# Zero matmuls ahead of the first transposes of a hybrid attention layer, and a first phase in program order

## The chip, the cores and the metric

The kernel runs on one core of a Trainium2 chip. The metric is the device time of one launch, in microseconds. The core's engines are TensorE (PE: matmuls and transposes; its weight loads are listed apart as PEld), VectorE (DVE), ScalarE (ACT), GpSimd (POOL) and SyncE (SP, which here issues most DMAs). Each engine works through a list of its own in order; they meet through semaphores, which are counters that one raises and another waits on.

## The reference, cut to what matters

One layer over 1024 positions of width 1024. The input is normed and multiplied with a wide weight matrix, eight heads of differential attention and four heads of gated linear attention work on the parts, and an output projection, a second norm and the residual follow:

```
h = rms_norm(x, pre_g)
z = jnp.einsum('bsd,de->bse', h, w_in)          # 1024 x 1024 by 1024 x 7184
qa, ka, va, ga, qb, kb, vb, gb, gk_low = split_columns(z)
...                                             # diff. attention -> oa, gated linear attention -> ob
y = jnp.einsum('bse,ed->bsd', jnp.concatenate([oa, ob], axis=-1), w_out)
return x + rms_norm(y, post_g)
```

All is float32. Only the first line and the start of the second are touched by the change.

## The kernel before, in words

**Loads.** SP first issues four tiles of x (`load_x`, L477: 128 rows by 1024 each), the gains `pre_g`, two raw weight pieces (`load_raw`, L194), the other four x tiles (named xt), two more raw pieces and two "early" pieces (`load_early`, L236).

**Norm.** For each of the first four x tiles `norm_x` lets ScalarE square the tile and sum (L491, "junk"), ScalarE and VectorE compute the reciprocal root (`rstd`, L1480 to L1490), VectorE scales the left half of the tile (L482), and POOL later scales the right half.

**Transposes.** `first(0)` transposes the left halves of the four x tiles on TensorE (L120): each x tile gives four blocks of 128 by 128, one into each of four PSUM banks ("xT"), so that a bank is full after the fourth x tile. Then `put` makes two numbers of each bank: `h_hi` on ScalarE (L521; rounded to TensorE's fast float32 form) and `h_lo` on VectorE (L522; the rest). POOL adds both to `f1hi` (L542). `first(1)` does the same for the right halves. Weights are split in the same way: `w` by ScalarE (L315, a cast) and by VectorE (L316, the rest).

**Products.** The input projection is done as a scheme of seven products of half matrices in place of eight. `order` lists them as (pair of weight columns, number of the product); `go(n)` runs the next n through `step` and `multiply`. One product is 24 matmuls of 256 columns for the wide pairs, in three groups of eight: h_hi by w's first part, h_hi by w's second part, h_lo by w's first part, into one PSUM bank. ScalarE copies the first sum away (L427, `s`), VectorE adds pairs of sums (L403, `gv_st`). The first product is (0, 1); it needs h_hi of the first half, k = 0 to 3, one after another. After the first four products `blocks(j)` transposes the xt tiles, which POOL has scaled by then (L482 with xt), makes h_hi, h_lo (L521, L522) and their sums and differences (L565 `s`, L568, L569, L548) for the next products.

**What sets the order.** TensorE's instructions are kept in program order by `mm` and `tr` (L117 and L120 are their lines, so all matmuls carry L117 and all transposes L120). In `norm_x` for the first four tiles the other engines are kept in program order too (`pin`). Everything else on ScalarE, VectorE and POOL is ordered by a scheduler, ahead of the run. The weights of products 0 to 3 are held behind the first norm (`issue_after`, in `prepare`). PSUM banks come from the list `free`: `take_bank` takes from its front, a finished bank is appended at its end.

Of the kernel before, what the change touches and what calls it, by code (L numbers as in the profile page):

```python
# [19 lines left out]
HB = 4  # L20
# [4 lines left out]
LAM_INIT = 0.2  # L25
# [6 lines left out]
def hymba_kernel(  # L32
# [18 lines left out]


    nc = tc.nc
    act, dve, pool, pe, sp = nc.scalar, nc.vector, nc.gpsimd, nc.tensor, nc.sync

    def fp(t):
        return t.bitcast(F32)

    def cols(half):
        return slice(half * 512, half * 512 + 512)  # L60


    const = ctx.enter_context(tc.tile_pool(name="const", bufs=1))
    pre_g = const.tile([P, KT], F32, name="pre_g")
# [4 lines left out]
    ones = const.tile([P, P], F32R, name="ones")  # L69
    pool.memset(fp(ones), 1.0)  # L70

    NZ = 512
    maskt = const.tile([P, NZ + P], F32, name="maskt")
    pool.memset(maskt, 0.0)
# [6 lines left out]
    sub_g = const.tile([P, 1], F32, name="sub_g")  # L81
# [34 lines left out]
    def mm(*a, **k):  # L116
        tc.keep_in_program_order(pe.matmul(*a, **k))  # L117

    def tr(dst, src):
        tc.keep_in_program_order(pe.transpose(dst, src, ident))  # L120

    edge = ctx.enter_context(tc.tile_pool(name="edge", bufs=1, side="right"))
    pool.memset(edge.tile([P, 120], F32, name="edge"), 0.0)
    hw = ctx.enter_context(tc.tile_pool(name="hw", bufs=1, side="right", reuse_waits="tile"))
    hpool_cm = tc.tile_pool(name="hpool", bufs=1, side="right")
    hpool = hpool_cm.__enter__()

# [16 lines left out]
    def at(part, j):  # L146
        per = HB // len(part)
        return part[j // per][:, j % per]
# [32 lines left out]
    def wide(p):  # L181
        return pairs[p][0] in ("VA", "VB")
# [18 lines left out]
    n_early = len(order)  # L201
# [15 lines left out]
    i = order.index((1, 4))  # L217
# [19 lines left out]

    def prepare(i):

        if i >= len(order) or i in ws:  # L240
            return
        if i < 4:

            act_ins, dve_ins = normed[0][:2]
            with tc.issue_after(act_ins.ins), tc.issue_after(dve_ins.ins):
                make_weights(i)
        else:
            make_weights(i)
# [97 lines left out]

    decs = {}
# [132 lines left out]
    def scale_x(st, cs, engine=pool):  # L480
        x_cs = xs[st][:, cs]
        return engine.tensor_scalar(x_cs, x_cs, norms[st], 1.0, ALU.mult, ALU.mult)  # L482

    norms, normed = {}, []

    def norm_x(*sts):
        n = len(sts)
        ssq = const.tile([P, 4, n], F32, tag=f"ssq{sts[0]}", name="ssq", bufs=1)
        for i, st in enumerate(sts):
            junk = hw.tile([P, D], F32, tag=("s2_hi0", "s2_lo0")[st % 2], name="junk")  # L490
            ins = act.activation(  # L491
                junk, xs[st], AF.Square, scale=D**-0.5, accum_out=ssq[:, 0, i : i + 1]
            )
            if n == 1:
                tc.keep_in_program_order(ins)
        pin = tc.keep_in_program_order if n == 1 else None
        normed[:] = [rstd(nc, ssq[:, :, :n], ssq[:, 0, :n], eps_t, pin)]
        for i, st in enumerate(sts):
            norms[st] = ssq[:, 1, i : i + 1]
            if n == 1:  # L500
                pin(scale_x(st, cols(0), dve))
            else:
                scale_x(st, slice(0, D))

# [14 lines left out]
    def put(ps, k, dst, j):  # L519
        hi, lo = dst  # L520
        act.activation(at(hi, j), ps, AF.Copy, scale=pre_g[:, k : k + 1])  # L521
        dve.scalar_tensor_tensor(  # L522
            at(lo, j), ps, pre_g[:, k : k + 1], fp(at(hi, j)), ALU.mult, ALU.subtract
        )
# [4 lines left out]
    def first(h):  # L529

        ps = [take_bank([P, 512], "xT") for _ in range(HB)]
        for i in range(4):
            for j in range(HB):
                k = h * HB + j
                tr(ps[j][0][:, i * P : (i + 1) * P], xs[i][:, k * P : (k + 1) * P])
        hi, lo = H[("h11", "h12")[h]]
        for j in range(HB):
            put(ps[j][0], h * HB + j, (hi, lo), j)
            if h:
                act.activation(f1[h][:, j], ps[j][0], AF.Copy, scale=pre_g[:, h * HB + j : h * HB + j + 1])  # L540
            else:
                pool.tensor_tensor(f1[h][:, j], fp(at(hi, j)), fp(at(lo, j)), ALU.add)  # L542
            free.append(ps[j][1])
# [51 lines left out]
    def go(n):  # L595
        for _ in range(n):
            i = made[0]
            if i == len(order):
                return
            made[0] = i + 1  # L600
            for a in range(4):
                prepare(i + a)
            step(i)
            if order[i][0] > EARLY and not (wide(order[i][0]) and order[i][0] % 2):
                wo_step(order[i][1])
            if fill and next(fill[0], 0) == 0:
# [12 lines left out]
    for j in range(HB):  # L619
        blocks(j)  # L620
        go(1)
# [96 lines left out]


    sp.dma_start(sub_g, attn_subln_g[0].rearrange("(p o) -> p o", o=1))  # L720
    dve.tensor_scalar(sub_g, sub_g, 1.0 - LAM_INIT, None, ALU.mult)
# [255 lines left out]
    def pin(first, ins):  # L977

        if first:
            tc.keep_in_program_order(ins)  # L980
# [545 lines left out]
```

## Time and profile before

| what | us |
| --- | --- |
| median of 3 runs | 979.86 |
| lowest and highest of these | 979.69, 980.12 |
| the profiled execution, its own time | 979.08 |
| span of the profiled execution | 977.4 |
| TensorE busy, of the span | 956.7 (98%) |
| VectorE busy | 735.4 (75%) |
| ScalarE busy | 600.5 (61%) |
| POOL busy | 142.9 (15%) |

The profile is of one execution. Its views used here: the page's head (busy time of each engine); the chain that ended last, followed back from the end; the same chain in order of time (start, length, what); the timeline (start, length, engine, line, operation, out<-in, count, and in brackets the idle time before it with what ended it); the groups by form (busy time, mean ns of one, idle before); and the windows (busy time and count in stretches, the granted TensorE clock as a share of full, the DMA share, GB/s). A line such as L521 is line 521 of the kernel before; after the change the same lines stand lower.

### The profile page before, as it was taken

The page shows a single profiled execution, that of the slowest core. Times are in us where ns is not written, and L with a number is a line of the kernel's source. Part 1 is how long each engine was busy: PE and PEld are TensorE (multiplying, and loading weights), DVE is VectorE, ACT ScalarE, POOL GpSimd, SP SyncE. Part 2 cuts the span into 40 slices and gives each one's busy share as a digit, 9 for nine tenths or more (in the row PEclk, how much of TensorE's full clock was granted, in tenths as well). Part 3 has the DMA queues.
Part 4 walks back from the last instruction along what each step waited for, and adds up shares of the span by engine and source line. Part 5 has one row for each costly group of instructions (what it writes and reads, how often), then busy time and mean ns, then how long its engine had stood idle before and what let it go on. Part 6 is the DMA issues. An engine that isn't in the chain of part 4 may idle for free.

```text
span 977.4 us, 15766 instructions
## 1 busy us (share of the span) xinstructions
PE 956.7 (98%) x5338; PEld 830.4 (85%) x5338; DVE 735.4 (75%) x1452; ACT 600.5 (61%) x1164; POOL 142.9 (15%) x158
## 2 busy tenths in 40 slices
PE   5999999999999999999999999999999999999997
PEld 5998988888889998999888888878888888888785
DVE  6887597789866667686786876487888888898554
ACT  8742455487357455454665775366776687887773
POOL 4300000000000010000200002121322222443321
PEclk9999999999999999999999999999999999999999
DMA  9432446656774868897987866987656669994677
GB/s 345 151 110 91 139 135 205 231 179 225 238 247 162 264 187 286 254 294 229 293 259 243 273 202 191 407 269 272 197 186 228 240 199 344 340 294 105 151 208 147
DMA packets 152593, 220.45 MB, mean 226 GB/s; under 512 B 17104, under 2 KB 83664, under 8 KB 152416
## 3 DMA queue, kind: packets, MB, share of 16 engines
q1 hardware_dynamic: 146176, 203.71, 64.1%
q0 software_dynamic: 6336, 15.73, 7.0%
q8 instruction: 42, 0.69, 0.3%
q14 instruction: 39, 0.32, 0.1%
HBM read 133.93 MB, written 88.60 MB: 228 GB/s over the span
## 4 chain that ended last, share of the span: by engine, by line
PE 95%; DVE 2%; ACT 1%; DMA 1%; issue 1%; POOL 0%; SPq 0%; DVEq 0%; ACTq 0%; POOLq 0%
PE x L117 24%; PE y L117 15%; PE z L117 15%; PE ypart L117 13%; PE sc L117 7%; PE po L117 5%; PE yps L117 4%; PE wtr L120 3%; PE gpo L117 3%; PE kv L117 1%; PE gkl_ps L117 1%; PE pa L117 1%; DMA x<-in_x_dram 1%; PE xT L120 1%; DVE s_lo L548 0%
## 5 line engine op out<-in xcount | busy, mean ns | idle before, releaser
L315 ACT CAST w<-w_raw 128x512 fp32r<-128x512 f32 (+1 forms) x164 | 112.4, 688 | 94.7 <-PE y L117 44.1
L316 DVE TENSOR_TENSOR w<-w_raw,w 128x512 fp32r<-128x512 f32 (+1 forms) x164 | 126.7, 774 | 50.1 <-ACT w L315 43.3
L1049 ACT ACTIVATE p<-p,stt 128x896 f32<-128x896 f32 (+7 forms) x128 | 99.3, 777 | 36.7 <-DVE stt L1039 33.9
L427 ACT COPY s<-x 128x512 f32<-128x512 f32 x84 | 49.1, 585 | 84.4 <-PE x L117 84.3
L775 POOL TENSOR_SCALAR_AFFINE_SELECT gan<-gan 128x512 f32<-128x512 f32 x8 | 16.5, 2060 | 485.4 <-ACT gan L774 449.8
L296 DVE TENSOR_TENSOR w_raw<-w_raw 128x512 f32<-128x512 f32 (+1 forms) x96 | 75.9, 791 | 13.9 <-DMA w_raw<-in_w_in_dram 12.6
L1039 DVE CUSTOM_DVE_ANT_0 p<-sc,maskt 128x512 f32<-128x512 f32 (+3 forms) x128 | 74.3, 585 | 14.5 <-PE sc L117 13.3
L117 PE MATMUL ypart<-wo_hi,m_hi 128*128 128x512 f32 x192 | 79.5, 414 | 0.1
L117 PE MATMUL y<-h_hi,w 128*128 128x512 f32 x320 | 79.6, 391 | 0.0
L117 PE MATMUL z<-s_hi,w 128*128 128x512 f32 x320 | 79.6, 391 | 0.0
L117 PE MATMUL x<-s_hi,w 128*128 128x512 f32 x320 | 79.6, 391 | 0.0
L1055 POOL TENSOR_SCALAR p<-p,stt,lam 128x1024 f32<-128x1024 f32 (+3 forms) x64 | 56.2, 879 | 146.9 <-DVE stt L1054 141.9
L117 PE MATMUL ypart<-wo_hi,m_lo 128*128 128x512 f32 x192 | 75.5, 393 | 0.0
L117 PE MATMUL ypart<-wo_lo,m_hi 128*128 128x512 f32 x192 | 75.4, 393 | 0.0
L117 PE MATMUL sc<-k,q 128*128 128x512 f32 (+1 forms) x192 | 69.0, 363 | 1.3 <-DVE stt L1039 1.2
L117 PEld LDWEIGHTS x<-s_hi,w 128*128 128x128 f32 x320 | 59.7, 188 | 12.2
L117 PEld LDWEIGHTS y<-h_hi,w 128*128 128x128 f32 x320 | 59.6, 188 | 12.2
L117 PEld LDWEIGHTS z<-s_hi,w 128*128 128x128 f32 x320 | 59.5, 188 | 12.0
L117 PE MATMUL sc<-ks,q 128*128 128x512 f32 (+1 forms) x192 | 66.1, 347 | 0.0
L1097 ACT CAST wt_hi<-wtr 128x512 fp32r<-128x512 f32 (+1 forms) x80 | 42.7, 534 | 24.6 <-PE wtr L120 23.8
L1098 DVE TENSOR_TENSOR wt_lo<-wtr,wt_hi 128x512 fp32r<-128x512 f32 (+1 forms) x80 | 50.7, 633 | 8.6 <-ACT wt_hi L1097 8.0
L1058 DVE SCALAR_TENSOR_TENSOR p<-p,stt,p 128x1024 f32<-128x1024 f32 (+3 forms) x64 | 52.1, 814 | 4.1 <-POOL p L1055 3.9
(226 smaller groups left out, 2247.7 us busy)
## 6 DMA issues: line engine op xcount, KB each, us to landing
w_raw<-in_w_in_dram SPq DMA_DIRECT2D x56, 512.0 KB, 4.7
wo_raw<-in_w_out_dram SPq DMA_DIRECT2D x32, 256.0 KB, 3.0
wo_d<-wo_hi SPq DMA_DIRECT2D x32, 256.0 KB, 2.8
wo_d<-wo_raw SPq DMA_DIRECT2D x32, 256.0 KB, 3.8
q<-q_d SPq DMA_DIRECT2D x32, 256.0 KB, 4.7
k<-k_d SPq DMA_DIRECT2D x32, 256.0 KB, 5.7
ks<-k_d SPq DMA_DIRECT2D x64, 128.0 KB, 6.2
v<-v_d SPq DMA_DIRECT2D x16, 512.0 KB, 7.0
```

Of the source, the lines that this page charges most:

```text
L117: tc.keep_in_program_order(pe.matmul(*a, **k))
L120: tc.keep_in_program_order(pe.transpose(dst, src, ident))
L296: dve.tensor_tensor(dst, a, b, ALU.subtract)
L315: act.copy(w[0], src)
L316: dve.tensor_tensor(w[1], src, fp(w[0]), ALU.subtract)
L427: act.copy(b[k], ps)
L1039: ins = dve.tensor_tensor_reduce(p[:, a:e], sc[:, : e - a], maskt[:, NZ + P - (e - a) :] if last else maskt[:, : e - a], 1.0, 3e38 if i == ...
L1049: act.activation(p[:, :n], p[:, :n], AF.Exp, bias=st[:, m : m + 1], scale=-1.0, accum_out=st[:, 2 + m : 3 + m],)
L1055: pool.tensor_scalar(p1[:, :n], p1[:, :n], st[:, 5:6], lam, ALU.mult, ALU.mult)
L1058: dve.scalar_tensor_tensor(p0[:, :n], p0[:, :n], st[:, 4:5], p1[:, :n], ALU.mult, ALU.subtract)
L1097: act.copy(hi[:, :n], pt[:, :n])
L1098: dve.tensor_tensor(lo[:, :n], pt[:, :n], fp(hi[:, :n]), ALU.subtract)
```

## The change

First, TensorE gets matmuls whose result nobody reads, of a tile of ones (weights) and a tile of zeros, `idle`, 512 columns each, through a new function `spin`: ten ahead of the first transpose, then 4, 8, 4 and 5 behind the transposes of the four x tiles, and one behind every second matmul of the first eight of the first product. They go into the PSUM bank at the end of the list `free`.

Second, a wrapper (`Queue`) around ScalarE, VectorE and POOL keeps each of their instructions in program order while `pinned` is set: from the first norm to the end of `put` in `first(1)`. The norms of xt (`norm_x(4, 5)` and `norm_x(6, 7)`) and the first product move ahead of `first(1)`; the weights of products 0 to 3 are made ahead of `first(0)`; those of products 4 to 10 are held behind the last pinned instruction of ScalarE and VectorE. POOL's memsets of `ones` and `idle` become its first, and the pools `edge` and `hw` are made earlier.

In the instruction lists of the two built programs TensorE's differ by the 35 spins alone, SP's not at all, POOL's by the order of its memsets and the one for `idle`. ScalarE's and VectorE's hold the same instructions; some stand a few places from where they were, nearly all of them within the first sixty or so. Since all three engines now pass through the wrapper, their instructions carry the wrapper's line (L66) after the change, matmuls L141 and transposes L144.

```
+    pinned = [False]
+    class Queue:
...
+            def run(*a, **k):
+                ins = op(*a, **k)
+                if pinned[0]:
+                    tc.keep_in_program_order(ins)
+                    self.last = ins.ins
+                return ins
...
+    act, dve, pool = Queue(nc.scalar), Queue(nc.vector), Queue(nc.gpsimd)
...
+    ones = const.tile([P, P], F32R, name="ones")
+    pool.memset(fp(ones), 1.0)
+    idle = hw.tile([P, 512], F32R, tag="s1_hi0", name="idle")
+    pool.memset(fp(idle), 0.0)
...
-        if i < 4:
-            act_ins, dve_ins = normed[0][:2]
-            with tc.issue_after(act_ins.ins), tc.issue_after(dve_ins.ins):
+        if 4 <= i <= n_early:
+            with tc.issue_after(act.last), tc.issue_after(dve.last):
                 make_weights(i)
...
+    def spin(n):
+        for _ in range(n):
+            ps = bank(free[-1], [P, 512], "spin")
+            mm(ps, ones, idle, start=True, stop=True)
...
                         stop=(j == 2 and k == HB - 1), skip_group_check=True,
                     )
+                if i == 0 and j == 0:
+                    spin(1)
...
+    pinned[0] = True
     for st in range(4):
         norm_x(st)
...
         ps = [take_bank([P, 512], "xT") for _ in range(HB)]
+        if not h:
+            spin(10)
         for i in range(4):
             for j in range(HB):
                 k = h * HB + j
                 tr(ps[j][0][:, i * P : (i + 1) * P], xs[i][:, k * P : (k + 1) * P])
+            if not h:
+                spin((4, 8, 4, 5)[i])
         hi, lo = H[("h11", "h12")[h]]
         for j in range(HB):
             put(ps[j][0], h * HB + j, (hi, lo), j)
+        pinned[0] = not h
+        for j in range(HB):
...
-    prepare(0)
+    for i in range(4):
+        prepare(i)
     first(0)
-    for i in range(1, 4):
-        prepare(i)
-    go(1)
-    first(1)
-    go(2)
     norm_x(4, 5)
     norm_x(6, 7)
     go(1)
+    first(1)
+    go(3)
     for j in range(HB):
         blocks(j)
         go(1)
```

More of the change, by code (lines that the diff above doesn't have):

```diff
@@ L53, in hymba_kernel, with __init__, __getattr__ @@
     nc = tc.nc
-    act, dve, pool, pe, sp = nc.scalar, nc.vector, nc.gpsimd, nc.tensor, nc.sync
+    pe, sp = nc.tensor, nc.sync
+    pinned = [False]
+    class Queue:
+        def __init__(self, engine):
+            self.engine = engine
+        def __getattr__(self, name):
+            op = getattr(self.engine, name)
+            def run(*a, **k):
[4 more added lines that the diff above has]
+                return ins
+            return run
+    act, dve, pool = Queue(nc.scalar), Queue(nc.vector), Queue(nc.gpsimd)
     def fp(t):
@@ L60, in cols @@
         return slice(half * 512, half * 512 + 512)
+    edge = ctx.enter_context(tc.tile_pool(name="edge", bufs=1, side="right"))
+    hw = ctx.enter_context(tc.tile_pool(name="hw", bufs=1, side="right", reuse_waits="tile"))
     const = ctx.enter_context(tc.tile_pool(name="const", bufs=1))
+    ones = const.tile([P, P], F32R, name="ones")
+    pool.memset(fp(ones), 1.0)
+    idle = hw.tile([P, 512], F32R, tag="s1_hi0", name="idle")
+    pool.memset(fp(idle), 0.0)
+    pool.memset(edge.tile([P, 120], F32, name="edge"), 0.0)
     pre_g = const.tile([P, KT], F32, name="pre_g")
@@ L68, in hymba_kernel @@
     pool.memset(eps_t, EPS)
-    ones = const.tile([P, P], F32R, name="ones")
-    pool.memset(fp(ones), 1.0)
     NZ = 512
@@ L120, in tr @@
         tc.keep_in_program_order(pe.transpose(dst, src, ident))
-    edge = ctx.enter_context(tc.tile_pool(name="edge", bufs=1, side="right"))
-    pool.memset(edge.tile([P, 120], F32, name="edge"), 0.0)
-    hw = ctx.enter_context(tc.tile_pool(name="hw", bufs=1, side="right", reuse_waits="tile"))
     hpool_cm = tc.tile_pool(name="hpool", bufs=1, side="right")
@@ L482, in scale_x @@
         return engine.tensor_scalar(x_cs, x_cs, norms[st], 1.0, ALU.mult, ALU.mult)
-    norms, normed = {}, []
+    norms = {}
     def norm_x(*sts):
@@ L490, in norm_x @@
             junk = hw.tile([P, D], F32, tag=("s2_hi0", "s2_lo0")[st % 2], name="junk")
-            ins = act.activation(
+            act.activation(
                 junk, xs[st], AF.Square, scale=D**-0.5, accum_out=ssq[:, 0, i : i + 1]
             )
[L494 to L497, printed above, removed]
+        rstd(nc, ssq[:, :, :n], ssq[:, 0, :n], eps_t, tc.keep_in_program_order)
         for i, st in enumerate(sts):
@@ L500, in norm_x @@
             if n == 1:
-                pin(scale_x(st, cols(0), dve))
+                scale_x(st, cols(0), dve)
             else:
@@ L720, in hymba_kernel @@
     sp.dma_start(sub_g, attn_subln_g[0].rearrange("(p o) -> p o", o=1))
-    dve.tensor_scalar(sub_g, sub_g, 1.0 - LAM_INIT, None, ALU.mult)
+    tc.keep_in_program_order(dve.tensor_scalar(sub_g, sub_g, 1.0 - LAM_INIT, None, ALU.mult))
     sp.dma_start(gla_g, gla_norm_g[0].rearrange("(t p) -> p t", p=P))
```

## The prediction

> **What bounds the kernel now.** I read the page's head and its chain first, then the chain in order of time over the first 45 us, then TensorE's waits there.
>
> ```profile
> span 977.4 us, 15766 instructions
> PE 956.7 (98%) x5338; PEld 830.4 (85%) x5338; DVE 735.4 (75%) x1452; ACT 600.5 (61%) x1164; POOL 142.9 (15%) x158
> PE 95%; DVE 2%; ACT 1%; DMA 1%; issue 1%; POOL 0%; SPq 0%; DVEq 0%; ACTq 0%; POOLq 0%
> ```
>
> TensorE holds 95% of the chain that ends last. Whatever makes its first product end later or earlier moves the end of the kernel, unless a later wait of TensorE takes it up.
>
> ```profile
> 12.17 0.50 DVE x L482
> 12.67 0.04 issue
> 12.71 0.91 PE xT L120 x3
> 13.63 0.05 issue
> 13.68 0.69 ACT h_hi L521
> 14.37 0.04 issue
> 14.41 5.76 PE x L117 x24
> 20.17 1.75 PE xT L120 x16
> 21.91 2.88 PE x L117 x24
> 24.79 5.76 PE y L117 x48
> ...
> 38.91 2.89 PE y L117 x24
> 41.80 0.02 issue
> 41.83 0.69 DVE gv_st L403
> ```
>
> (Start us, length us, what.) Before 14.41 each x tile is squared, scaled and transposed; from 14.41 to 41.80 the chain is TensorE alone. The first product (24 matmuls of 256 columns) takes 5.76 us, 0.24 each; the same product in its next turn takes 2.88, 0.12 each. The 16 transposes at 20.17 take 0.11 each, the first ones about 0.22. So TensorE runs at half its rate up to about 19.8 us. The clock column doesn't show it: it says 1.00 in both of the first rows here (stretch, us, TensorE busy, clock, DMA share, GB/s), though the matmuls in 2 us (the x) go from 10 to 20.
>
> ```profile
> 16.40:18.40 2.00, 2.00 (x10) 1.00 1.06 381
> 21.80:23.80 2.00, 2.00 (x20) 1.00 1.40 455
> ...
> 975.00:976.00 1.00, 0.00 (x0) 0.00 (x0) 0.00 (x0) 0.00 (x0) 0.00 (x0) 0.77 0.60 229
> ```
>
> The column does fall at the other end, within 975 to 976, some 5 us after the last matmul. I call the two rates cold and warm. Warm came 5.4 us after the product's start at 14.41.
>
> **The change part by part: where the first product can end.** The other engines set a floor:
>
> ```profile
> 11.60 2.17 ACT L315 CAST w<-w_raw 128x1024 fp32r<-128x1024 f32 x2
> 12.66 2.77 DVE L316 TENSOR_TENSOR w<-w_raw,w 128x1024 fp32r<-128x1024 f32 x2
> 13.68 2.42 ACT L521 ACTIVATE h_hi<-xT,pre_g 128x512 fp32r<-128x512 f32 x4
> 15.35 2.71 DVE L522 SCALAR_TENSOR_TENSOR h_lo<-xT,pre_g,h_hi 128x512 fp32r<-128x512 f32 x4
> ```
>
> ScalarE's casts hold it until about 13.7, so faster transposes alone don't start h_hi earlier. VectorE is busy without a gap from 12.66 to 18.06, when the fourth h_lo is done. Both lists are in the same order in the changed program. A warm product could thus end at 18.06 plus two matmuls and a little, 18.4, against 20.17 now: 1.8 us is all that warmth can give.
>
> **The spins are not a dense stream.** In the built program each of the 31 spins before the product (10, then 4, 8, 4, 5 after the four groups of transposes) waits on TensorE's own counter for the spin before it, because all are new tiles in one bank:
>
> ```
> Matmult spin_277<-idle_66,ones_64 128x512 [waits Pool >= 2]
> Matmult spin_279<-idle_66,ones_64 128x512 [waits PE >= 1]
> Matmult spin_281<-idle_66,ones_64 128x512 [waits PE >= 2]
> ...
> Matmult x_393<-w_265,h11_hi_179 128x256
> Matmult spin_396<-idle_66,ones_64 128x512 [waits DVE >= 22]
> ```
>
> No matmul of before waits for one just ahead of it, so I bound the step of such a spin.
>
> ```profile
> 961.68 0.39 PE L117 MATMUL yps<-wo_hi,m_hi 128*128 128x512 f32 x1
> 961.91 0.39 PE L117 MATMUL yps<-wo_hi,m_lo 128*128 128x512 f32 x1
> ...
> L117 PE MATMUL x<-w,h_lo 128*128 128x256 f32 x6 | 1.5, 415 | 0.0
> L117 PE MATMUL x<-w,h_hi 128*128 128x256 f32 x1 | 0.6, 583 | 0.6 <-ACT h_hi L521 0.6
> ...
> L117 PE MATMUL y<-w,h_lo 128*128 128x256 f32 x8 | 1.1, 283 | 0.0
> L117 PE MATMUL y<-w,h_hi 128*128 128x256 f32 x1 | 0.4, 356 | 1.3 <-DVE s L565 1.3
> ```
>
> Low end: the wait costs nothing, and a 512-column spin takes the 0.227 us between starts of the first two rows (0.45 cold). High end: it waits for the whole length of the one before, starts from a standstill, and pays the 0.04 to 0.05 us between engines in the chain. Warm that is 0.39 + 0.07 (356 against 283 ns after a wait) + 0.04 = 0.50 us. Cold: 256 more columns cost 0.39 - 0.28 = 0.11 warm, so 0.22 cold; 0.415 + 0.22 + 0.165 (583 against 415) + 0.04 = 0.84 us. I take the high end: a wait on a counter that is raised at a matmul's end is nearest to these rows of matmuls after a wait.
>
> Start of the spins: ones and idle are now POOL's first memsets.
>
> ```profile
> 0.81 0.20 POOL masks.py:197 MEMSET ident<- 128x128 f32 x1 [0.29 <-POOLq L1512]
> ...
> 31.43 0.53 POOL L652 MEMSET ku<- 128x512 f32 x1
> ```
>
> 0.81 + 0.20 + 0.53 gives 1.5 us. With the 5.4 us above, warm comes at 6.9: six to seven cold spins, then 3.6 at 0.50, and the ten end at 8.7. From there I step on, four warm transposes being 0.45 us: first tile done 9.15; four spins (2.0), second tile 11.6; eight spins (4.0), third 16.05; four (2.0), fourth 18.5. Before, the fourth was done at 13.63. ScalarE's h_hi x4 (2.42) then runs to 20.95; h_lo starts after the first h_hi, 19.2, and ends 2.71 later, at 21.9.
>
> **The spins inside the product.** They go into the bank last freed, that of the fourth transposed tile; its last reader is the fourth h_lo, VectorE's instruction 22. So after two matmuls TensorE stands until 21.9 (in before's timing until 18.06). Behind it stand the other 22 matmuls. Three rounds of a spin and two matmuls at 0.50 (the spin's own wait is just longer than 0.23 + 0.24), one spin at 0.23 and 16 matmuls at 0.12 make 3.65: the product ends at 25.6, which is 5.4 us later than 20.17.
>
> By the Trainium skill ("TensorE: Matmul & The Clock Gate", Part 1: the HAM clock gate) the clock is given at the end of a busy window of 3.4 us that runs free of the kernel, so warm would come anywhere from 4.9 to 8.3 instead of 6.9; estimated from that page, the ten spins would end at 7.9 to 9.3, and the sum would move by -0.8 to +0.6. The trace's 5.4 us lies within one to two such windows.
>
> **What else moves.** The squares of the last four x tiles (ScalarE, L491) and their small VectorE operations go ahead of the copy of the first sum and of the second h_hi.
>
> ```profile
> 24.42 5.41 POOL L482 TENSOR_SCALAR xt<-xt,ssq 128x1024 f32<-128x1024 f32 x4 [2.25 <-ACT h_hi L521]
> 16.17 5.99 POOL L542 TENSOR_TENSOR f1hi<-h_hi,h_lo 128x512 f32<-128x512 f32 x4 [2.95 <-DVE h_lo L522]
> ```
>
> This lets POOL scale xt straight after f1hi: with h_lo from 19.2, 6.0 + 5.4 ends near 31.5. TensorE wants xt at 30.55 + 5.4 = 36, so cover is 4.5 us (0.7 in before); without it TensorE would wait for xt. The second h_hi and h_lo come while TensorE does 1.75 + 2.88 us of transposes and product: cover again; uncovered, they would cost at most those 2.4 to 2.7 us. The memsets and ident (needed 7.21 before) hide under the wait for x, and the one added memset's 0.53 would otherwise be paid. SP's queue holds the same instructions in the same order; no DMA is moved past another. VectorE's list changes at one place that TensorE waits for:
>
> ```profile
> 41.83 0.69 DVE L403 TENSOR_TENSOR gv_st<-y,s 128x512 f32<-128x512 f32 x1 [0.16 <-PE y L117]
> 42.44 0.74 DVE L522 SCALAR_TENSOR_TENSOR h_lo<-xT,pre_g,h_hi 128x512 fp32r<-128x512 f32 x1
> 43.09 0.74 DVE L565 SCALAR_TENSOR_TENSOR s<-xT,pre_g,h 128x512 f32<-128x512 f32 x1
> 43.98 2.15 PE L117 MATMUL y<-w,h_hi 128*128 128x256 f32 x16 [1.32 <-DVE s L565]
> ```
>
> VectorE waits 0.16 for gv_st's bank, then does 0.65 of it, and only then the two that TensorE awaits. In the changed list h_lo and s stand ahead of gv_st: 0.8 of the 1.32 us goes (bounds 0 and 1.3); what is late next is s itself. The other exchanged neighbours on VectorE and ScalarE I cost at nothing, under a TensorE that is busy from there on; a missed one costs one operation, 0.7.
>
> **Sum.** +5.4 - 0.8 = +4.6 us. The profiled execution took 979.08 us (1.7 outside the span), so 983.7; it lies 0.8 below the median of 979.86, so the measured median should be 984.5, 0.5% slower. Its own bounds, 981.5 to 987, come from when warm is reached and from a handoff or restart that is half or one and a half times as dear over 20 spins.
>
> **The rivals.**
>
> Spins never warm the array (990 to 996.5). Standing spins keep it streaming for 0.45 of 0.84 us, about half. For it: before 14.41 TensorE was busy in bursts and stayed cold, and the paced start of the product did not warm it at once. Against it: its records would be nearly gapless. All 31 spins at 0.84, or 0.63 without the restart, and four cold groups at 0.9 take TensorE to 31.1 or 24.6; the product (7.6 cold, 1.1 less once warm 5.4 us in) ends at 37.6 or 31.1: +17.4 or +10.9, less 0.8. A clock that comes and goes gives something between 987 and that. The Trainium skill names this ("TensorE: Matmul & The Clock Gate", A second HAM failure mode: psum-queue depth-cycling): idle moments between matmuls make the clock swing between its two rates.
>
> The own wait costs nothing (980.5). Spins at 0.227 fit into the gaps between the x tiles (four in 0.9, eight in 1.8); nothing is late up to 14.41. The stand until 18.06 is left, then 3.55: end at 21.6, +1.4 - 0.8. For it: the counts fit those gaps so closely. Against it: the list of waits.
>
> Faster (977.3). The same, and the bank's wait falls away too: the product ends at 18.4, and -1.8 - 0.8 = -2.6. It decides where the product ends before about 19.0, and needs the spin after the second matmul not to stand for VectorE; the list says that it does.
>
> **How the numbers follow.** Forecast 0.43, cold spins 0.33 (there the change doesn't do what it says), free wait 0.18, faster 0.06. A measurement here tells about 0.2% (2.0 us) from no change: below 977.9 is faster, above 981.8 slower. Slower: 0.40 + 0.33 + 0.01 = 0.74; same: 0.03 + 0.16 = 0.19; faster 0.07. The range goes from 979.5, which leaves out the faster case, to 993.5, which leaves out the dearer third of cold spins.
>
> **What would show it.** Spin starts 0.5 apart warm and 0.84 cold (0.227: free wait); the fourth tile's transposes ending near 18.5, not 13.6; a TensorE wait for h_lo in the product; its end near 25.6; the wait for s near 0.5 us. Wrong would be: spins without a stand between them, or cold matmuls still after 25 us.

## The result, and the profile after

The median went from 979.99 us (979.69 to 980.48) to 994.74 (992.69 to 996.66), four runs of each: a ratio of 1.015 [1.0129, 1.0171]. The forecast was 984.5 with a range up to 993.5, so the sign was right and the time lies beyond the range. It is near what the first rival, spins that never warm the array, gave: 996.5.

The profiled execution of the changed kernel took 992.69 us, 13.6 more than the 979.08 of the one before. The head of its page (span; busy time and count of each engine):

```profile
span 991.0 us, 15837 instructions
PE 978.0 (99%) x5373; PEld 838.9 (85%) x5373; DVE 737.6 (74%) x1452; ACT 601.1 (61%) x1164; POOL 142.1 (14%) x159
```

TensorE's busy time grew by 21.3 us, the span by 13.6. A higher busy share is no good sign here: the added 35 matmuls count as work.

The same chain in order of time, after (start us, length us, what):

```profile
1.49 0.04 issue
1.53 0.81 PE spin L141
2.34 0.04 issue
2.38 0.81 PE spin L141
...
29.63 0.43 PE x L141 x2
30.06 0.43 PE spin L141
...
31.89 0.24 PE x L141 x2
...
32.45 1.91 PE x L141 x16
34.37 1.75 PE xT L144 x16
```

Before, this chain began with the work on the x tiles and reached the first product at 14.41. Now it begins with the spins. One spin begins every 0.85 us: 0.81 and an "issue" of 0.04, in which TensorE waits for nothing that the profile shows but its own spin before. The first product ends at 34.37, not 20.17: 14.2 us later. The pair of x matmuls at 29.63 takes 0.43, the one at 31.89 takes 0.24: the array is cold until about 31.2 us, where before it was warm from 19.8. (The trace also holds a record of the clock: full rate begins at 31.22 us there, at 19.81 in before.)

TensorE's timeline, after (start, length, engine, line, operation, out<-in, count, and in brackets the idle time before it with its releaser):

```profile
1.53 8.47 PE L141 MATMUL spin<-idle,ones 128*128 128x512 f32 x10 [1.53 <-POOL idle L66]
9.80 1.05 PE L144 MATMUL xT<-ident,x 128*128 128x128 f32 x4
10.51 3.33 PE L141 MATMUL spin<-idle,ones 128*128 128x512 f32 x4
...
25.44 4.19 PE L141 MATMUL spin<-idle,ones 128*128 128x512 f32 x5
29.43 0.63 PE L141 MATMUL x<-w,h_hi 128*128 128x256 f32 x2
29.86 0.63 PE L141 MATMUL spin<-idle,ones 128*128 128x512 f32 x1
...
57.09 2.15 PE L141 MATMUL y<-w,h_hi 128*128 128x256 f32 x16 [0.23 <-DVE s L66]
```

No gap is shown between the spins, and none of the groups of transposes waits for VectorE any more: the x tiles are ready long before TensorE comes to them. The last row is the matmul that waited 1.32 us for s before. It starts 13.1 us later, with 0.23 of that wait left, so 1.1 of the 14.2 had come back by there. A wait for a weight (w), which before did not have, takes 0.7 again:

```profile
PE x L141 <- DVE w L66: 0.7, 1, 0.7
```

(Who waits for whom: us in total, times, longest.) That makes the distance 13.8; at the end it is 13.6.

### The profile page after: what moved, and what is told of

It reads as the page before. It is cut to its first block, busy times and chain, and to the rows that moved or that the text cites. A ratio compares the mean times of both kernels' runs of the same rounds, so it can differ in the third digit from the quotient of the medians.

```text
span 991.0 us, 15837 instructions
## 1 busy us (share of the span) xinstructions
PE 978.0 (99%) x5373; PEld 838.9 (85%) x5373; DVE 737.6 (74%) x1452; ACT 601.1 (61%) x1164; POOL 142.1 (14%) x159
## 4 chain that ended last, share of the span: by engine, by line
PE 95%; DVE 2%; issue 1%; ACT 1%; POOL 0%; DVEq 0%; POOLq 0%; ACTq 0%
PE x L141 23%; PE z L141 15%; PE y L141 15%; PE ypart L141 13%; PE sc L141 7%; PE po L141 5%; PE yps L141 4%; PE wtr L144 3%; PE gpo L141 3%; PE spin L141 3%; PE kv L141 1%; PE gkl_ps L141 1%; PE pa L141 1%; PE xT L144 1%; DVE s_lo L66 1%
## 5 line engine op out<-in xcount | busy, mean ns | idle before, releaser
L66 ACT CAST w<-w_raw 128x512 fp32r<-128x512 f32 (+1 forms) x164 | 112.4, 688 | 94.9 <-PE y L141 45.7
L66 DVE TENSOR_TENSOR w<-w_raw,w 128x512 fp32r<-128x512 f32 (+1 forms) x164 | 126.4, 773 | 51.3 <-ACT w L66 45.1
L66 ACT ACTIVATE p<-p,stt 128x896 f32<-128x896 f32 (+7 forms) x128 | 99.3, 777 | 35.6 <-DVE stt L66 34.5
L66 ACT COPY s<-x 128x512 f32<-128x512 f32 x84 | 49.2, 585 | 89.1 <-PE x L141 88.9
L66 POOL TENSOR_SCALAR_AFFINE_SELECT gan<-gan 128x512 f32<-128x512 f32 x8 | 17.2, 2154 | 485.5 <-ACT gan L66 485.5
L66 DVE CUSTOM_DVE_ANT_0 p<-sc,maskt 128x512 f32<-128x512 f32 (+3 forms) x128 | 74.3, 585 | 15.3 <-PE sc L141 14.1
L66 DVE TENSOR_TENSOR w_raw<-w_raw 128x512 f32<-128x512 f32 (+1 forms) x96 | 75.4, 786 | 13.2 <-DMA w_raw<-in_w_in_dram 11.9
L141 PE MATMUL y<-h_hi,w 128*128 128x512 f32 x320 | 79.7, 391 | 0.0
L141 PE MATMUL z<-s_hi,w 128*128 128x512 f32 x320 | 79.6, 391 | 0.0
L141 PE MATMUL ypart<-wo_hi,m_hi 128*128 128x512 f32 x192 | 79.5, 414 | 0.1
L141 PE MATMUL x<-s_hi,w 128*128 128x512 f32 x320 | 79.6, 391 | 0.0
L66 POOL TENSOR_SCALAR p<-p,stt,lam 128x1024 f32<-128x1024 f32 (+3 forms) x64 | 56.2, 879 | 146.3 <-DVE stt L66 144.0
L141 PE MATMUL ypart<-wo_hi,m_lo 128*128 128x512 f32 x192 | 75.5, 393 | 0.0
L141 PE MATMUL ypart<-wo_lo,m_hi 128*128 128x512 f32 x192 | 75.4, 393 | 0.0
L141 PEld LDWEIGHTS x<-s_hi,w 128*128 128x128 f32 x320 | 59.7, 188 | 12.2
L141 PEld LDWEIGHTS y<-h_hi,w 128*128 128x128 f32 x320 | 59.6, 188 | 12.2
L141 PE MATMUL sc<-k,q 128*128 128x512 f32 (+1 forms) x192 | 68.9, 363 | 1.0 <-DVE stt L66 1.0
L141 PEld LDWEIGHTS z<-s_hi,w 128*128 128x128 f32 x320 | 59.4, 188 | 12.0
L141 PE MATMUL sc<-ks,q 128*128 128x512 f32 (+1 forms) x192 | 66.0, 347 | 0.0
L66 ACT CAST wt_hi<-wtr 128x512 fp32r<-128x512 f32 (+1 forms) x80 | 42.8, 535 | 25.5 <-PE wtr L144 24.7
L66 DVE TENSOR_TENSOR wt_lo<-wtr,wt_hi 128x512 fp32r<-128x512 f32 (+1 forms) x80 | 50.6, 632 | 8.8 <-ACT wt_hi L66 8.1
L66 DVE SCALAR_TENSOR_TENSOR p<-p,stt,p 128x1024 f32<-128x1024 f32 (+3 forms) x64 | 52.1, 813 | 4.1 <-POOL p L66 3.9
```

The costliest lines, as they stand in the source:

```text
L66: ins = op(*a, **k)
```

## The experiments

**The theories.** Standing: a spin that waits for the spin just ahead keeps the array streaming for only half the time, which is too little to earn the faster clock; so the price is the wait, not the zeros. Zeros: a product of zeros warms nothing, however dense. And beside both: the reordering of the other engines (the second half of the change) may itself cost something. Ratios are to the kernel before on the same chip; "second transposes" is the start of the 16 transposes behind the first product in the timeline, which measures that product's end (before 20.01, after 34.20).

| kernel | second transposes, us | median, us (lowest to highest) | ratio |
| --- | --- | --- | --- |
| the change | 34.20 | 994.74 (992.69 to 996.66) | 1.0150 [1.0129, 1.0171] |
| e1, one tile for each call | 21.61 | 982.72 (981.37 to 984.62) | 1.0034 [1.0023, 1.0044] |
| e2, the same in a bank of its own | 18.49 | 979.54 (978.11 to 982.65) | 0.9997 [0.9986, 1.0008] |
| e3, no spins | 19.21 | 979.53 (978.61 to 981.69) | 1.0001 [0.9992, 1.0010] |
| e4, a tile for each pair | 23.45 | 984.11 (983.61 to 985.15) | 1.0044 [1.0029, 1.0059] |
| e5, e2 with none in the product | 17.91 | 979.57 (978.61 to 981.12) | 1.0002 [0.9993, 1.0011] |
| e6, before and spins alone | 20.29 | 984.40 (982.12 to 985.89) | 1.0048 [1.0032, 1.0064] |
| e7, two banks by turns | 18.53 | 979.29 (978.41 to 980.77) | 0.9999 [0.9990, 1.0008] |
| e8, dense lead, then standing spins | 22.96 | 982.37 (981.67 to 982.77) | 1.0026 [1.0016, 1.0036] |
| e9, e5 with f1hi late | 17.92 | 985.16 (980.77 to 986.63) | 1.0060 [1.0046, 1.0073] |
| e10, e9 with 13 leading spins | 17.88 | 983.50 (982.88 to 984.21) | 1.0040 [1.0028, 1.0053] |
| e11, e3 with f1hi late | 18.41 | 982.71 (980.82 to 983.43) | 1.0027 [1.0016, 1.0039] |
| e12, e5 with 13 leading spins | 17.96 | 981.00 (978.98 to 983.00) | 1.0009 [0.9999, 1.0018] |

**e1: the same spins, but those of one call share a tile**, so that only the first of a call has a wait.

```
-        for _ in range(n):
-            ps = bank(free[-1], [P, 512], "spin")
+        ps = bank(free[-1], [P, 512], "spin")
+        for _ in range(n):
             mm(ps, ones, idle, start=True, stop=True)
```

> The spins of one call share one tile, so that none waits for the spin just before it; the spins in the product still go into the bank of the fourth transposed tile. Standing theory (spins that wait for each other leave the array idle for half the time, which doesn't earn the clock): spins start 0.43 apart while cold and 0.23 once warm, warm comes between 5 and 11 us, the fourth tile is transposed by 13.7 to 15, TensorE then stands in the product until the fourth h_lo near 18 to 19.5, and the product ends at 21.6 if the clock stays through that stand, near 25 if it falls; 980.5 to 984 us in all. Rival (a product of zeros into an unread bank never earns the clock, however dense): 31 spins at 0.43 with cold transposes, product end near 28, 987 us.

TensorE's timeline of e1:

```profile
1.53 4.63 PE L141 MATMUL spin<-idle,ones 128*128 128x512 f32 x10 [1.53 <-POOL idle L66]
...
12.52 0.60 PE L144 MATMUL xT<-ident,x 128*128 128x128 f32 x4
...
17.69 0.50 PE L141 MATMUL spin<-idle,ones 128*128 128x512 f32 x1 [1.82 <-DVE h_lo L66]
...
21.61 1.91 PE L144 MATMUL xT<-ident,x 128*128 128x128 f32 x16
```

Ten spins take 4.63 us in place of 8.47, and the third group of transposes is already warm (0.60 for four, cold 1.05). So zeros do warm the array, and the theory of zeros falls. The spin behind the first two matmuls of the product now stands 1.82 us for the fourth h_lo, the wait that the prediction had read off the list. In the changed kernel it doesn't show, because TensorE begins the product only at 29.43, when the fourth h_lo is done (28.64). The first product of e1 ends 1.6 us later than before: the stand for the bank costs what the warmth brings, and more. The rest of the 0.34% (3.1 us of the medians) comes later. At the awaited y product the profiled execution is only 0.2 us behind (44.19 against 43.98); then TensorE waits 1.3 for w and 0.9 for gu near 410 us, and the end is 2.9 later. The four longest of the ten executions (984.03 to 984.62) also have a lower mean granted clock, 0.995 to 0.996 against 0.998 to 0.999, so there the clock was down for some more microseconds; where is not on record.

**e2: as e1, in bank 7, which nobody else uses yet.**

```
+        ps = bank(7, [P, 512], "spin")
```

> As the one-tile version, and all spins go into a bank that no transposed tile uses, so those in the product don't wait for VectorE. Standing theory: warm as there, no stand in the product, which ends one or two matmuls behind the fourth h_lo, at 18.4 to 19; 977 to 978.5 us, faster than before by about 2. Rival (zeros never earn the clock): product end near 27, 986 us.

TensorE's timeline of e2:

```profile
18.49 1.91 PE L144 MATMUL xT<-ident,x 128*128 128x128 f32 x16
...
43.19 2.15 PE L141 MATMUL y<-w,h_hi 128*128 128x256 f32 x16 [1.46 <-DVE s L66]
```

The first product ends 1.5 us earlier than before, near the floor of 18.4 that the prediction worked out. But the median is that of before: the expectation missed by 1 to 2.5 us. (The interval of the ratio, 0.9986 to 1.0008, leaves room for a gain of up to 1.4 us.) At 43 us 0.8 of the 1.5 is left, and the wait for s is 1.46 long, not shorter.

**e3: no spins, the second half of the change alone** (the body of `spin` is `pass`).

> All spins left out; the program order of the first phase and the moved calls stay. Both theories: cold first product 14.4 to about 20.2, the wait of TensorE for s shorter by 0.6 to 1.1 us; 979.0 to 979.5 us. A third, that the new order itself costs, would show more than 980.5.

```profile
13.47 4.24 PE L141 MATMUL x<-w,h_hi 128*128 128x256 f32 x16 [0.46 <-ACT h_hi L66]
...
43.19 2.15 PE L141 MATMUL y<-w,h_hi 128*128 128x256 f32 x16 [1.32 <-DVE s L66]
```

The reordering alone starts the first product 0.9 us earlier (14.41 before) and the awaited y product 0.8 earlier (43.98 before), and the end doesn't move by more than the noise: 1.0001 [0.9992, 1.0010], that is within 1 us. So the 14.8 us of the change are the spins', to within that 1 us. The wait for s is no shorter than before (1.32), against the expectation: in this kernel's list gv_st still stands ahead of h_lo and s (VectorE does it at 41.03, s at 42.30), where in the change it stands behind them (56.87, s at 56.21). And e3 reaches the y product at the very time of e2, though e2's first product ended 0.7 sooner.

**e4: a new tile for every second spin.**

```
-        for _ in range(n):
-            ps = bank(free[-1], [P, 512], "spin")
+        for m in range(n):
+            if m % 2 == 0:
+                ps = bank(free[-1], [P, 512], "spin")
```

> Two spins to a tile: the second of a pair doesn't wait, the next pair does. A pair should take 0.43 + 0.85 = 1.28 us cold and stream for 0.85 of it, two thirds. Standing theory with a bar between one half and two thirds: warm before 14 us, the fourth tile's transposes by 15 to 17, 981 to 985 us. With a bar above two thirds, or by the rival that zeros never count: all pairs cold, product end near 31, 990 us.

Its timeline:

```profile
1.53 6.34 PE L141 MATMUL spin<-idle,ones 128*128 128x512 f32 x10 [1.53 <-POOL idle L66]
...
15.73 0.60 PE L144 MATMUL xT<-ident,x 128*128 128x128 f32 x4
```

A pair takes about 1.25 us, of which it streams 2 x 0.43: two thirds. By the trace's clock record the array was warm from 10.9 us, not within the 6.3 us of the ten spins. An estimate from these rows: 68% wasn't enough during the ten spins; the 3.4 us before 10.9, with four cold transposes (0.21 each) packed beside four spins, streamed for some 2.9 us, and that was.

**e5: e2 without the spins inside the product** (the call `spin(1)` in `multiply` goes).

> The one-tile version in bank 7 (979.54 us, first product ended near 18.5) without the four spins inside the first product. TensorE-bound theory: the four spins cost 0.9 us of the product, which should now end at the fourth h_lo, 17.6 to 18, and the whole should be 0.5 to 0.9 shorter, 978.7. VectorE-bound theory (from about 18 to 59 us VectorE is busy without a gap, so what TensorE gains turns into a wait for s near 43 us): the product ends earlier, the wait for s grows by as much, and the time stays at 979.5.

```profile
17.91 1.91 PE L144 MATMUL xT<-ident,x 128*128 128x128 f32 x16
...
26.14 0.50 PE L141 MATMUL y<-w,h_lo 128*128 128x256 f32 x2 [0.16 <-DVE h_lo L66]
...
43.09 2.15 PE L141 MATMUL y<-w,h_hi 128*128 128x256 f32 x16 [1.46 <-DVE s L66]
```

The first product ends 2.1 us earlier than before, and the y product starts at 43.09, as in e2 (43.19) and e3 (43.19). Three kernels whose first products end 1.3 us apart meet again there, behind the same instruction of VectorE. How busy VectorE is, from the windows of the 55 us from 11 to 66 (the sum over them, first of before, then of e5):

```profile
sum 55.00, PE 52.40 PEld 50.01 DVE 50.95 ACT 39.62 POOL 15.69; mean PE 6.55 PEld 6.25 DVE 6.37 ACT 4.95 POOL 1.96
```

```profile
sum 55.00, PE 53.11 PEld 50.03 DVE 53.44 ACT 39.01 POOL 13.19; mean PE 6.64 PEld 6.25 DVE 6.68 ACT 4.88 POOL 1.65
```

VectorE is busy 53.44 of 55 us, as much as TensorE. Over the whole span it is the second engine with 75%; in this stretch it is a bound of its own. (In e3 it is not quite so: there VectorE waits 0.16 us for TensorE ahead of gv_st at 41.03.)

**e6: the other half alone**, the kernel before with early memsets and 31 dense spins in bank 7, without the reordering.

```
+    def spin(n):
+        ps = bank(7, [P, 512], "spin")
+        for _ in range(n):
+            mm(ps, ones, idle, start=True, stop=True)
...
+        if not h:
+            spin(10)
...
+            if not h:
+                spin((4, 8, 4, 5)[i])
```

> Before, with nothing added but the 31 spins outside the product, one tile to a call, in bank 7: no wrapper, no moved calls, VectorE in nearly the order of before. Product end near 18 to 18.5. If the moved and pinned VectorE work (two subtractions of raw weights that before does at 19 and 22 us now come after 26) is what eats the gain of the one-tile version: 977.5 to 978.3 us. If VectorE bounds the stretch up to 59 us in any order: 979.0 to 979.6.

ScalarE's timeline of e6 has the square of an xt tile ahead of the awaited h_hi:

```profile
15.11 1.05 ACT L498 ACTIVATE junk<-xt 128x1024 f32<-128x1024 f32 x1
```

What TensorE waits for there:

```profile
16.88 2.61 PE L121 MATMUL x<-w,h_hi 128*128 128x256 f32 x14 [0.68 <-ACT h_hi L528]
...
32.24 0.33 PE L124 MATMUL xT<-ident,xt 128*128 128x128 f32 x1 [1.18 <-POOL xt L489]
33.34 0.76 PE L124 MATMUL xT<-ident,xt 128*128 128x128 f32 x5 [0.77 <-POOL xt L489]
```

Both theories' numbers missed: it is 0.48% slower. Adding spins changed the scheduler's order on the other engines: the square delays the next h_hi by 1 us and TensorE by 0.68, and POOL scales the last xt tiles so late that TensorE waits twice for them, 1.18 and 0.77. What the reordering is good for is seen here: it keeps these places fixed. It has no gain of its own (e3), but without it the spins disturb the rest. By there e6 is 2.7 us behind before; the profiled execution ends 4.5 behind, and the other 1.8, lost after 400 us, was not followed up. The kernel therefore doesn't isolate the spins.

**e7: as many waits as in the change, but on the spin before last**: every spin a new tile, in banks 6 and 7 by turns.

```
+            turn_of[0] ^= 1
-            ps = bank(free[-1], [P, 512], "spin")
+            ps = bank(6 + turn_of[0], [P, 512], "spin")
```

> The spins as in the changed kernel, each a new tile with a wait on TensorE's counter, but in banks 6 and 7 by turns, so that each waits for the spin before last; none touches the bank of a transposed tile. Standing theory (what counts is waiting for the one just ahead): 0.43 apart cold, 0.23 warm, warm by 6 to 11 us, product end near 18.5 to 19, 979.5 us. Rival (any wait on a counter stops the stream): 0.6 or more apart, 984 or more.

```profile
1.53 4.63 PE L141 MATMUL spin<-idle,ones 128*128 128x512 f32 x10 [1.53 <-POOL idle L66]
...
18.53 1.91 PE L144 MATMUL xT<-ident,x 128*128 128x128 f32 x16
```

Same spins, same tiles, one more bank: the ten leading spins take 4.63 us in place of 8.47, and the median is 15.4 us below the changed kernel's (979.29 against 994.74). It is not the semaphores that cost, nor the tiles, but waiting for the matmul just ahead.

**e8: 16 dense spins first, then spins that stand for each other** between the transposes, in bank 7; none in the product. This asks whether a standing stream that can't earn the clock can keep it.

```
+        if n == 16:
+            ps = bank(7, [P, 512], "spin")
+            for _ in range(n):
+                mm(ps, ones, idle, start=True, stop=True)
+            return
         for _ in range(n):
-            ps = bank(free[-1], [P, 512], "spin")
+            ps = bank(7, [P, 512], "spin")
```

> Sixteen dense spins ahead of the first transpose, so that the array is warm when it starts, then the 21 spins between the transposes wait for each other as in the changed kernel; none in the product. If standing spins keep a clock that dense ones have earned (as the prediction's forecast assumed of them): 0.50 apart throughout, the fourth tile transposed near 16.5, 982 to 983 us. If they lose it: 0.85 apart again within some 4 to 8 us of the last dense one, the fourth tile near 20 to 22, 986 to 988.

```profile
10.63 4.38 PE L141 MATMUL spin<-idle,ones 128*128 128x512 f32 x8
14.85 0.60 PE L144 MATMUL xT<-ident,x 128*128 128x128 f32 x4
...
22.96 1.91 PE L144 MATMUL xT<-ident,x 128*128 128x128 f32 x16
```

It can. Eight standing spins take 4.38 us, some 0.53 each, and the transposes behind them stay warm (0.60). Each of these spins streams for 0.21 of 0.53 us, about 40%, less than the 50% that did not earn the clock in the change. So earning and keeping have different bars. This kernel is also the forecast's own scene, a warm array with standing spins: the product ended 2.95 us later than before, and the profiled execution took 2.6 more (the median 2.9).

**e9 to e11: is it POOL's sums (f1hi) that keep VectorE slow from 17 to 24 us?** In e5, beside these sums, a tiny operation of VectorE on ssq (128 by 2) takes 1.1 us, as much as the split of a whole weight later on (VectorE's timeline of e5):

```profile
18.30 1.12 DVE L1515 TENSOR_TENSOR ssq<-ssq 128x2 f32<-128x2 f32 x1
...
27.14 1.22 DVE L66 TENSOR_TENSOR w<-w_early,w 128x1024 fp32r<-128x1024 f32 x1
```

POOL's timeline of e5:

```profile
15.62 5.03 POOL L66 TENSOR_TENSOR f1hi<-h_hi,h_lo 128x512 f32<-128x512 f32 x4 [2.95 <-DVE h_lo L66]
```

So f1hi is moved behind the scaling of xt, with the spins of e5 (e9), with 13 leading spins (e10), and without spins (e11).

```
-            else:
-                pool.tensor_tensor(f1[h][:, j], fp(at(hi, j)), fp(at(lo, j)), ALU.add)
...
     norm_x(6, 7)
+    f1_sums()
     go(1)
```

> The one-tile version in bank 7 without spins in the product (979.57 us), with POOL's four f1hi sums moved behind its scaling of xt. In that version VectorE's small operations of the norms (128x2) took up to 1.1 us each between 18 and 23 us while POOL did f1hi, against 0.15 otherwise, and VectorE was busy 53.4 of 55 us up to 66. VectorE-bound theory: with POOL idle there, VectorE saves 2 to 4 us, h_lo of the second half follows h_hi at once, the wait for s near 43 us shrinks, and of the 2.2 us that the first product gained 1.5 to 2 reach the end: 977.5 to 978.5 us. Rival (what is gained is lost further on, in the stretch of 400 to 540 us where transfers run at 0.8 to 0.9 of the queues' capacity): the lead at 60 us grows, and the time stays at 979 to 979.6.

> The same with 13 spins ahead of the first transpose in place of 10, so that dense work lasts from 1.5 to about 7.1 us whatever the phase of the window in which the clock is decided. If the executions of the ten-spin versions differ because warm comes at 6 to 7 us in some and at 10 to 11 in others, the spread of the executions shrinks and the median falls by 0.3 to 0.8 against the ten-spin version; if not, the first transposes start up to 0.3 late and the median is the same.

> No spins, and POOL's f1hi behind the scaling of xt. VectorE-bound theory: the cold product still ends near 20, but the wait for s near 43 us shrinks by 0.5 to 1.3: 978.3 to 979. If the rival of the first holds, 979.5 as without the move.

All three missed. In e5 the tiny operations were not slow in themselves: each ends within 0.02 us of the operation of POOL that runs beside it (19.42 and 19.40, 20.67 and 20.65 during the sums; 22.16 and 22.15, 23.25 and 23.25 during the scaling of xt), so it stood for POOL. From e9's timelines of POOL, VectorE and TensorE:

```profile
24.04 8.01 POOL L66 TENSOR_TENSOR f1hi<-h_hi,h_lo 128x512 f32<-128x512 f32 x4
```

```profile
18.07 0.16 DVE L1519 TENSOR_TENSOR ssq<-ssq 128x2 f32<-128x2 f32 x1 [0.33 <-ACT ssq L1512]
...
26.35 2.31 DVE L66 TENSOR_TENSOR w<-w_early,w 128x1024 fp32r<-128x1024 f32 x1
```

```profile
45.00 2.15 PE L141 MATMUL y<-w,h_hi 128*128 128x256 f32 x16 [2.85 <-DVE s L66]
```

The tiny operations are short now (0.16), but POOL's sums run beside VectorE's large ones: 2.31 us for the split of a weight in place of 1.22 in e5, and a mean of 2.0 for the four sums in place of 1.26. Single records show them taking turns: a sum of POOL from 25.29 to 27.58, the split from 26.35 to 28.66, the next sum from 27.55 to 29.81, each ending some 1.1 us after the one before it. VectorE meets two such splits, and s comes 1.9 us later (45.00 against 43.09). Moving an operation of POOL moves the collision, it doesn't remove it. In e10 and e11 something follows from the stand of 2.85 (42.12 to 44.97 in e10). TensorE's windows in e10 (stretch, us, busy and count, granted clock, DMA share, GB/s):

```profile
40.00:43.00 3.00, 1.73 (x14) 1.00 0.00 0
43.00:44.00 1.00, 0.00 (x0) 0.90 0.00 0
44.00:48.00 4.00, 3.03 (x14) 0.50 0.19 66
48.00:50.00 2.00, 2.00 (x11) 0.50 0.00 0
50.00:52.00 2.00, 2.00 (x10) 0.84 0.00 0
52.00:56.00 4.00, 4.00 (x19) 1.00 0.19 66
```

The clock falls to half within the stand, at 43.8 us, and is back near 50.6, though TensorE was busy again from 45; between 45 and 55 us this kernel falls 2.5 us further behind before. In e11 the 16 matmuls behind the same stand take 3.47 us, in e9 2.15: there the clock did not fall in the profiled execution. But that is the shortest of e9's six (980.77). Four of the others, 984.88 to 986.63 us, have a mean granted clock of 0.994 or 0.995, as e10's profiled execution has, so the median of 985.16 is for the most part that of executions in which the clock fell; one (986.52, clock 0.999) is slow without it.

**e12: e5 with 13 leading spins instead of 10**, in case the moment at which warmth comes spreads the times.

> The one-tile version in bank 7 without spins in the product (979.57 us), with 13 spins in place of 10 ahead of the first transpose. In the profiles with ten dense spins warm came at 6.0 to 6.8 us in some and at 10.5 to 11.0 in others. If that is what spreads the executions of the ten-spin version (978.6 to 981.1), warm now comes by 8.3 at the latest, the highest execution falls to 980 and the median to 979.0 to 979.3. If VectorE bounds the stretch after it, or the spread has another source, median and spread stay.

981.00 (978.98 to 983.00), 1.0009 [0.9999, 1.0018]. The second transposes start at 17.96 and the y product at 43.14, as in e5, and the spread is not smaller. So the moment of warming is not what keeps the gain away.

## Why the prediction was wrong, point by point

**The step that failed** is "With the 5.4 us above, warm comes at 6.9". The 5.4 us was measured on before's product, where matmuls follow each other without a stand, and was carried over to a stream that the same text describes as standing half the time. The runs show in its place: cold spins at 0.85 stayed cold as long as there were only spins and transposes, and warmth came at 31.2 us, 1.8 after the product had begun; dense ones were warm by 6 to 11. All that was built on 6.9 fell with it: the ten spins ended at 10.0 (8.7 forecast), the fourth tile's transposes near 25.4 (18.5), the product at 34.37 (25.6). So the forecast had 5.4 of the 14.2 us; the other 8.8 is the array that stayed cold. That the sign was right doesn't bear out the account of the clock.

**Right:** that each spin waits for the one before (e7: the same number of waits, one spin further back, costs nothing); the cold step, 0.84 worked out, 0.85 measured; the warm step, 0.50 worked out, some 0.53 in e8; the first spin at 1.5; that the wait for s would shrink (1.32 to 0.23), with gv_st behind s as forecast, though its place is worth only some 0.6 of the 1.1 us (its step in VectorE's row) and what gave the rest was not followed; that the queues of SP and POOL cost nothing in the change (behind the first spin TensorE's waits name neither POOL nor a DMA).

**The terms of the rival that held** were somewhat too dear. The four groups of transposes were priced at 0.9 each and take 0.7 (10.51 less 9.80). The product was to take 6.5 us (37.6 less 31.1) and took 4.7 (34.37 less 29.63), since warmth came 1.8 us after its start and not 5.4. Together 2.6 us; the spins' 0.85 for 0.84 gives 0.3 back; some 1.0 more lies in the last spin of each of the five groups, whose successor starts 0.2 before it ends (9.80 against 1.53 + 8.47). 17.4 less these 3.3 is 14.1; 14.2 was measured.

**The sum's -0.8** was half right: 1.1 came back at s, and the wait for w took 0.7 of it again; by the end the distance is 13.6, a net -0.6.

**The stand for h_lo in the product**, until 21.9 in the forecast, is real (1.82 us in e1, 1.17 in e4), but in the change it has no time to show.

**The rival of a free wait** fell at its first step: the spins start 0.85 apart, not 0.45. e1 shows what it described, spins without a wait and a stand for the bank, and there its 21.6 for the product's end is met (21.61), but not its time: 982.72 us against 980.5.

**The rival "Faster"** named nearly the right floor: 18.4 for the product's end, 18.49 and 18.53 in e2 and e7. Without spins in the product (e5, e9, e10, e12) it ends at 17.9, because there the fourth h_lo is done by 17.5 and not 18.06. Its gain of 2.6 at the end did not come in any run. Part of the cause is shown: e2, e3, e5, e7 and e12 come to the awaited y product at 43.04 to 43.19 whatever their first product did; in e5 VectorE sets that. The lead of 0.8 to 0.9 over before that is left there is gone by the end of four of these five profiled executions; that of e3, the shortest of its twelve, keeps 0.5. In e2 it goes near 410 us, where VectorE waits 2.94 us for a raw weight from DMA and TensorE then 1.2 for VectorE:

```profile
408.86 1.23 DVE L66 TENSOR_TENSOR w_raw<-w_raw 128x1024 f32<-128x1024 f32 x1 [2.94 <-DMA w_raw<-in_w_in_dram]
```

In before it waited 0.82 there:

```profile
407.62 1.23 DVE L296 TENSOR_TENSOR w_raw<-w_raw 128x1024 f32<-128x1024 f32 x1 [0.82 <-DMA w_raw<-in_w_in_dram]
```

That is one profiled execution of each. It is so in e12 too, but not in e3, e5 and e7: followed matmul by matmul, e5 loses 0.9 between 508 and 610 us and e7 0.8 between 805 and 899. So what takes this last lead stays open. So do what exactly is counted as busy, and whether data other than zeros would have warmed the array sooner; neither was tried.

**The weights.** The rival had the right mechanism and 0.33. What spoke for it, half of the time streaming, was a number; what spoke against it, "nearly gapless" records, was how the profile draws a waiting matmul. The number should have had the larger chance.

## What to carry to other kernels

To warm TensorE with matmuls that nobody reads, let them run into each other: one tile for all, or two banks by turns; a new tile in the same bank makes each wait for the one ahead, which doubled the step here (0.46 to 0.85 us) and kept the clock down besides. Give them a bank that no other engine still reads. And before paying for an earlier first product, look for the next place where TensorE waits: here VectorE, busy for 53.4 of 55 us, gave the second stage its time, and a product 2.1 us earlier gained nothing that could be measured at the end (e5: 1.0002 [0.9993, 1.0011]).

## What the runs showed of the hardware

**Earning and keeping the clock differ.** Spins that streamed half of the time never earned it in 28 us, pairs at two thirds did not in six; spins that streamed 40% of the time kept it for 12 us in e8. In the profiled executions a stand of 1.82 us (e1) lost nothing; one of 2.85 lost the clock for 6.8 us in e10 (43.8 to 50.6), for 3.4 in e11 (44.5 to 47.9) and not at all in e9. The Trainium skill ("TensorE: Matmul & The Clock Gate", Part 1: the HAM clock gate) says that the clock is judged in windows of 3.4 us that run free of the kernel, and the clock records here agree: in before, the rise (19.8 us) and the fall (975.5) lie 955.73 us apart, 280 times 3.4133. By that rule alone a window that is busy half of the time might have gone either way; here it did not earn the clock. How full a window must be can be estimated from the traces: counted back from the rise in steps of 3.41 us, with 0.43 us of streaming for a cold spin and 0.21 for a cold transpose or product matmul, the window that ends in the rise is filled to 77% or more in all fourteen profiles (77% in the change and in e7), and every full window ahead of it to 73% or less (73% in e6). In the change none before 27.81 us has more than 67%.

**Phase.** The same ten dense spins from 1.53 us brought warmth at 6.5 us in e2, 6.8 in e7 and 10.5 in e1. By the count above the window from 3.05 us in e2 is filled to 85%, while e1's two, from 0.27 and from 3.68, get 58% and 67%: the spins last 4.6 us, and whether one window is filled by them depends on where it begins.

**The clock row of the page says 1.00 over the whole cold start**, in every run: the trace's clock record begins with the first rise, and what lies ahead of it reads as full. Later falls are shown, as in e10. At the start of a kernel the rate is read from the matmuls' lengths (0.81 a spin cold, 0.43 for a pair of x matmuls cold, 0.24 warm).

**POOL and VectorE can hold each other up** when both work on float32 tiles. In e5 an operation of VectorE on 128 by 2 numbers took 1.05 to 1.21 us, against 0.16 with POOL idle in e9, and ended with POOL's, whichever that was (a sum or the scaling of xt). In e9 the split of a weight took 2.31 us in place of 1.22 and three of POOL's four sums 2.27 to 2.29 in place of some 1.28, by turns. It is not so for every operation: h_lo, which reads PSUM, took 0.73 beside POOL's sums in e5 and 0.74 with POOL idle (at 36.02).
